# Weighting the last two thirds of a modulation on ScalarE and GpSimd instead of TensorE

## The chip, the cores and the metric

One core of one Trainium2 chip. The metric is device time in microseconds, the median over the runs shown. Engines are named as in the profile: PE (TensorE, matmuls; PEld its weight loads), DVE (VectorE), ACT (ScalarE), POOL (GpSimd), SP (SyncE, which issues most of the DMAs).

## The reference

One layer of a decoder trunk over 512 tokens of width 1024. A condition vector `c` gives six rows of 1024 numbers, the modulation; three token mixers (MLA, sliding window, NSA) run on the modulated, normalised input, then an output projection, a normalisation, and a mixture of 16 experts with two chosen for each token.

```python
cond = jax.nn.silu(c)
mod = cond @ ada_w[l] + ada_b[l]                 # (1, 6144); ada_w is (1024, 6144) f32
sh1, sc1, gt1, sh2, sc2, gt2 = jnp.split(mod[:, None, :], 6, axis=-1)
h = (_ln(x) * (1.0 + sc1) + sh1)
y = concat(o_a, o_b, o_c) @ w_out[l]             # MLA, window, NSA on h @ w_in
x = layernorm(ALPHA * x + (1.0 + gt1) * y, ln1_g[l], ln1_b[l])
h = (_ln(x) * (1.0 + sc2) + sh2)
y = moe(h, router_w, router_bias, ...)
x = layernorm(ALPHA * x + (1.0 + gt2) * y, ln2_g[l], ln2_b[l])
```

Counted in twelve blocks of 512 columns, blocks 0 to 3 are sh1 and sc1, 4 and 5 gt1, 6 and 7 sh2, 8 and 9 sc2, 10 and 11 gt2. Blocks 0 to 3 are needed at once; the change is about blocks 4 to 11, 16 MB of `ada_w`.

## The kernel before

Everything is f32 on tiles of 128 partitions. The program is a straight line without loops on the chip. A scheduler orders the instructions of each engine ahead of time, by the order in which they are written and by hand-set offsets of priority (the table PRM; `pri("st0")` and so on); on the chip each engine and each DMA queue then works its list strictly in order.

The work runs in this order: load x, normalise, transpose (to about 50 us); the first third of the modulation (lines 371 to 388); projections and MLA attention (`keysA`, `latA`, `mla`; about 50 to 130 us), with the projections C1 (`c1`) and B2 (`keys`) between; compression of NSA's keys (`cps`); window attention (`swa`); NSA attention (`queries`, `nsa`; about 200 to 345 us) with the output projection of the four token tiles (`outproj`, yps) between; routing of each tile (`route`, a long chain of small DVE instructions that ends in the table tokB); then four rounds of experts (gu, dn, cmb), whose rows are gathered through tokB by POOL's DMA queue.

The modulation's later blocks are a matrix-vector product on PE. `load_ada` brings 128 rows by 1024 columns at a time (512 KB) into a slot of the pool zraw, which has five slots that w_in's chunks (B2r, C2r ...), phi, w_out and others share. `gemv` (line 320) multiplies two such halves, each half of 512 columns on a quarter of the array, by a column of `cond` that is padded to 32 columns. A DVE addition (lines 537, 548) adds the bank to a row tile. Blocks 4 to 7 are `mod_steps` with four steps, blocks 8 and 9 two more steps of `mod_half`, blocks 10 and 11 two steps of `mod_half` again (`gsteps`). The steps of `mod_steps` are placed between MLA's tiles (line 674, five of the six) and in the order of NSA (s1, the sixth); `gsteps` run at line 1274, behind the output projection. `mod_cols` turns rows into columns by PE transposes, for sh2 and sc2; `gate_out` adds 1 to the gate rows and writes them to DRAM, from where `gate_in` spreads them over all partitions.

Of the kernel before, what the change touches and what calls it, by code (L numbers as in the profile page):

```python
# [10 lines left out]
F32 = mybir.dt.float32  # L11
# [3 lines left out]
OP = mybir.AluOpType  # L15
# [28 lines left out]
T, D, NT, KD = 512, 1024, 4, 8  # L44
# [64 lines left out]
def build(tc, A, out, dbg=None):  # L109
    nc = tc.nc  # L110
    V, S, G, PE, SP = nc.vector, nc.scalar, nc.gpsimd, nc.tensor, nc.sync
# [28 lines left out]
    with top:  # L140
# [3 lines left out]
        cst = top.enter_context(tc.tile_pool(name="cst", bufs=1))  # L144
# [6 lines left out]
        def wraw(name):  # L151
            return zraw.tile([128, 1024], F32, name=name, tag="w")

        def bank(tag, name, bufs=None):
            return psp.tile([128, 512], F32, name=name, tag=tag, bufs=1 if tag in "oq" else 2)
# [4 lines left out]
        gt_d = dram.tile([4, 512], F32, name="gt_d")  # L160
# [23 lines left out]
        for n in range(NT):  # L184
            SP.dma_start(x0[n], xv[:, n])

        def load_ada(i, k, half=(0, 1)):
            t = []
            for a in half:
                t.append(wraw(f"ada{i}_{k}{a}"))  # L190
                c = 2048 * i + 1024 * a
                SP.dma_start(t[-1], A["ada_w"][k * 128:(k + 1) * 128, c:c + 1024])
            return t

        w_in = A["w_in"].rearrange("(k p) c -> p k c", p=128)

        def raw_half(name, hf, ranges):
# [47 lines left out]
        ident = C("id")  # L245
# [66 lines left out]
        def together(calls):  # L312

            head = calls[0]()
            with tc.issue_after(head.ins), tc.high_priority():
                for c in calls[1:]:
                    head = c()
            return head

        def gemv(ps, tiles, first, last):  # L320
            def one(j):
                k, t = tiles[j // 2]
                return lambda: PE.matmul(ps[32 * j:32 * j + 32], cond[:, k], t[:, 512 * (j % 2):512 * (j % 2) + 512],  # L323
                                         start=first, stop=last, skip_group_check=True)


            together([one(j) for j in (2, 0, 1, 3)])

        def mod_bias(i, n=4):
            r = cst.tile([128, 512], F32, name=f"mod{i}", tag=f"mod{i == 8}", bufs=1)  # L330
            V.memset(r, 0.0)
            SP.dma_start(r[0:32 * n:32], A["ada_b"][i:i + n])
            return r

        def mod_cols(i, r):
            ps = bank("t", f"modt{i}")
            for s in range(4):
                PE.transpose(ps[:, s * 128:(s + 1) * 128], r[:, s * 128:(s + 1) * 128], ident)
            c = cst.tile([128, 4, 4], F32, name=f"modc{i}")
            V.tensor_copy(c, ps.rearrange("p (s q) -> p q s", s=4)[:, 0:128:32, :])  # L340
            return c

        def gate_out(i, r):
            V.tensor_scalar(r[0:64], r[0:64], 1.0, None, op0=OP.add)
            SP.dma_start(gt_d[2 * i:2 * i + 2], r[0:64:32])

        def gate_in(i, dst):
            SP.dma_start(dst, gt_d[2 * i:2 * i + 2].rearrange("(o a) c -> o (a c)", o=1).to_broadcast([128, D]))
# [178 lines left out]
        wukv = mp.tile([128, 512], F32, name="wukv", tag="wv")  # L527


        m1, m2 = mod_bias(4), mod_bias(8, 2)  # L530

        def mod_steps():
            for k in range(0, KD, 2):
                ps = bank("z", "modps1")
                for kk in (0, 1):
                    gemv(ps, [(k + kk, t) for t in load_ada(1, k + kk)], kk == 0, kk == 1)
                V.tensor_tensor(m1, ps, m1, op=OP.add)
                yield
            yield from mod_half(m2, 0)

        def mod_half(r, a):

            for k in range(0, KD, 4):
                ps = bank("z", "modps2")
                for kk in (0, 2):
                    gemv(ps, [(k + kk + i, load_ada(2, k + kk + i, (a,))[0]) for i in range(2)], kk == 0, kk == 2)
                for h in range(2):
                    V.tensor_tensor(r[0:64], ps[64 * h:64 * h + 64], r[0:64], op=OP.add)
                yield

        steps = mod_steps()

        def step(n, it=steps):
            for _ in range(n):
# [118 lines left out]
            with pri(f"st{n}"):  # L673
                step(pr(f"stn{n}", 1))
        chB2 = load_chunk("B2", (672, 928))
        mc1 = mod_cols(1, m1)
        gate_out(0, m1)
        zc = {"k": kp.tile([128, 16, 32], F32, name="zck"), "v": kp.tile([128, 16, 32], F32, name="zcv")}
        for kv in "kv":
            src = kr if kv == "k" else vc  # L680
# [289 lines left out]
                load_wo(a, b, wol[a][:, b])  # L970
        gt1 = wraw("gt1")
        gate_in(0, gt1)
        m3 = mod_bias(10, 2)
        gsteps = mod_half(m3, 1)

        def gstep(n):
            step(n, gsteps)
# [27 lines left out]
            return dst  # L1005


        ones = rp.tile([128, 128], F32, name="ones")
        V.memset(ones, 1.0)
        step(16)  # L1010
        mc2 = mod_cols(2, m2)
        V.tensor_scalar(mc2[:, 0:2], mc2[:, 0:2], 1.0, None, op0=OP.add)
        sc2 = lambda k: mc2[:, k // 4, k % 4:k % 4 + 1]
        sh2 = lambda k: mc1[:, 2 + k // 4, k % 4:k % 4 + 1]

        rwm = yp.tile([128, 2, KD, 16], F32, name="rwm")
        rw_ = rwm[:, 1]
# [4 lines left out]
        shr = rp.tile([128, 16], F32, name="shr")  # L1022
        rb05 = rp.tile([128, 16], F32, name="rb05")
        V.tensor_scalar(rb05, rbias, 0.5, None, op0=OP.add)
        for a, mc in enumerate((mc2[:, 0:2], mc1[:, 2:4])):
            V.tensor_tensor(rwm[:, a], rw_, mc.rearrange("p a b -> p (a b)")[:, :, None].to_broadcast([128, KD, 16]),
                            op=OP.mult)
        ps = bank("s", "rsum")
# [243 lines left out]
            G.memset(r, 0.0)  # L1272
        cnt_w = [0]
        step(16, gsteps)
        gate_out(1, m3)
        gt2 = wraw("gt2")
        gate_in(1, gt2)
        lg2 = ep.tile([128, D], F32, name="lg2", bufs=1)
# [266 lines left out]
```

## Time and profile before

| | |
|---|---|
| median of 3 runs | 598.21 us (597.69 to 601.78) |
| profiled execution, device time | 595.62 us |
| its span | 593.8 us |
| TensorE clock granted, mean | 0.97 |
| DMA moved in the span | 117.05 MB |

The span runs from the first to the last recorded instruction; the device time also holds what lies around it. A busy PE is a PE with a matmul in flight. A row of the timeline has start, duration, engine, line, operation; "x8" is a count of records, and an f32 matmul leaves two records.

### The profile page before, as it was taken

To read this page: it belongs to the slowest core of one execution; us is meant where nothing else is said; L and a number is where in the kernel's file an instruction comes from. 1 tells how busy PE (TensorE), PEld (TensorE's weight loads), DVE (VectorE), ACT (ScalarE), POOL (GpSimd) and SP (SyncE) were. 2 spreads that over 40 slices of the span, in tenths; PEclk is the share of its full clock that TensorE was granted. 3 is DMA by queue.
4 is the path that set the end of the run, shared out by engine and by line. 5 is a ranking of instruction groups with operands and counts; after the bars stand their busy time and mean duration, and the time that the engine had idled before them with its cause. 6 is when DMAs were issued, how large, how long until landed. Compare 5 with 4: busy or idle time off the path is not lost.

```text
span 593.8 us, 10447 instructions
## 1 busy us (share of the span) xinstructions
PE 546.8 (92%) x3856; PEld 328.6 (55%) x3856; DVE 367.4 (62%) x1218; ACT 221.8 (37%) x556; POOL 97.5 (16%) x114
## 2 busy tenths in 40 slices
PE   2899999999799999999899999788899999999990
PEld 1469675687698988754455456554334334234240
DVE  7635566654778569877769388885036266157274
ACT  2533543651447336475644412140442071070130
POOL 0214200000000010005101112231501222010123
PEclk9879999999899999999999999987999999999995
DMA  8994137834921100196300794558699999999601
GB/s 302 372 326 170 53 115 273 259 108 145 314 74 40 68 2 2 44 221 202 106 2 1 248 311 149 172 181 285 184 372 354 375 360 342 383 351 340 229 2 47
DMA packets 77546, 117.05 MB, mean 197 GB/s; under 512 B 7937, under 2 KB 54440, under 8 KB 77492
## 3 DMA queue, kind: packets, MB, share of 16 engines
q1 hardware_dynamic: 72328, 102.60, 53.2%
q0 software_dynamic: 4960, 13.64, 6.5%
q8 instruction: 32, 0.52, 0.4%
q14 instruction: 22, 0.18, 0.1%
q10 hardware_dynamic: 204, 0.11, 0.1%
HBM read 112.12 MB, written 8.40 MB: 203 GB/s over the span
## 4 chain that ended last, share of the span: by engine, by line
PE 76%; DVE 9%; DMA 5%; issue 4%; POOL 2%; ACT 2%; ACTq 0%; POOLq 0%
PE gu L1319 13%; PE zps L407 12%; PE dn L1367 7%; PE onsa L894 6%; PE yps L1215 5%; DMA ada<-in_ada_w_dram 3%; PE modps L323 3%; PE zall L423 3%; PE gTp L997 2%; PE stp L501 2%; PE sps L921 2%; PE cmb L1409 2%; PE modps L375 2%; PE wps L849 1%; PE warm L356 1%
## 5 line engine op out<-in xcount | busy, mean ns | idle before, releaser
L1319 PE MATMUL gu<-gu,gT 128*32 128x512 f32 x768 | 87.8, 604 | 0.1
L1319 PEld LDWEIGHTS gu<-gu,gT 128*32 128x32 f32 x768 | 23.2, 110 | 51.1 <-issue 47.9
L1367 PE MATMUL dn<-dn,aT 128*32 128x512 f32 x384 | 45.3, 597 | 0.4 <-ACT aT L127 0.2
L1002 ACT ACTIVATE gT<-gTp,modc,modc 128x128 f32<-128x128 f32 x96 | 35.6, 459 | 9.7 <-PE gTp L997 9.2
L1343 DVE TENSOR_TENSOR act<-act,gu 128x256 f32<-128x256 f32 x12 | 5.0, 421 | 52.4 <-ACT act L1342 52.4
L1215 PE MATMUL yps<-wol,oM 128*128 128x512 f32 x64 | 30.9, 595 | 0.0
L1342 ACT ACTIVATE act<-gu 128x256 f32<-128x256 f32 x12 | 4.6, 387 | 66.1 <-PE gu L1319 66.1
L1373 DVE SCALAR_TENSOR_TENSOR y<-dn,tab,gt 128x512 f32<-128x512 f32 x24 | 18.0, 749 | 16.9 <-PE dn L1367 16.4
L323 PE MATMUL modps<-ada,cond 128*32 128x512 f32 x128 | 18.3, 631 | 5.0 <-DMA ada<-in_ada_w_dram 4.9
L1367 PEld LDWEIGHTS dn<-dn,aT 128*32 128x32 f32 x384 | 10.3, 109 | 20.9 <-issue 16.2
L894 PE MATMUL onsa<-pt,vs 128*64 128x512 f32 x40 | 20.6, 614 | 0.0
L491 ACT ACTIVATE Sg<-Sg,nms 128x128 f32<-128x128 f32 (+3 forms) x32 | 17.8, 559 | 3.7 <-DVE nms L490 3.5
L491 ACT ACTIVATE W<-W,nmw 128x256 f32<-128x256 f32 (+1 forms) x32 | 15.3, 477 | 9.7 <-DVE nmw L490 9.3
L997 PEld LDWEIGHTS gTp<-cf,rows 128*128 128x128 f32 x96 | 10.4, 142 | 15.1 <-ACT gT L1002 9.2
L1389 ACT ACTIVATE R<-R,rsf 128x1024 f32<-128x1024 f32 x3 | 3.7, 1241 | 40.3 <-DVE rsf L1388 40.3
L448 DVE TENSOR_TENSOR rp<-zps,trig 128x128 f32<-128x128 f32 (+1 forms) x28 | 9.7, 346 | 12.6 <-PE zps L407 12.1
L997 PE MATMUL gTp<-cf,rows 128*128 128x128 f32 x96 | 14.8, 282 | 1.7 <-DMA rows<-xs_d,tokB 1.7
L356 PEld LDWEIGHTS warm<-cf 128*128 128x128 f32 x88 | 12.8, 207 | 6.3 <-issue 5.5
L127 ACT COPY pt<-stp 128x512 f32<-128x512 f32 x14 | 7.9, 586 | 22.2 <-PE stp L501 21.9
L356 PE MATMUL warm<-cf 128*128 128x128 f32 x88 | 16.1, 309 | 0.1
L407 PE MATMUL zps<-B1s,hH 128*128 128x256 f32 x64 | 14.1, 312 | 2.2 <-DVE B1s L210 1.1
L1377 DVE TENSOR_TENSOR ys<-y,ys 128x512 fp32r<-128x512 f32 x22 | 15.1, 686 | 1.0 <-ACT ys L127 0.7
(523 smaller groups left out, 1467.6 us busy)
## 6 DMA issues: line engine op xcount, KB each, us to landing
ada<-in_ada_w_dram SPq DMA_DIRECT2D x48, 512.0 KB, 5.9
gu<-in_moe_w_gate_dram SPq DMA_DIRECT2D x32, 512.0 KB, 9.7
gu<-in_moe_w_up_dram SPq DMA_DIRECT2D x32, 512.0 KB, 9.6
dn<-in_moe_w_down_dram SPq DMA_DIRECT2D x16, 1024.0 KB, 10.5
x<-in_x_dram SPq DMA_DIRECT2D x4, 512.0 KB, 5.1
phik<-in_nsa_phi_k_dram SPq DMA_DIRECT2D x4, 512.0 KB, 5.1
phiv<-in_nsa_phi_v_dram SPq DMA_DIRECT2D x4, 512.0 KB, 4.8
wo<-in_w_out_dram SPq DMA_DIRECT2D x8, 256.0 KB, 9.4
```

Source lines behind the costliest of these rows:

```text
L323: return lambda: PE.matmul(ps[32 * j:32 * j + 32], cond[:, k], t[:, 512 * (j % 2):512 * (j % 2) + 512], start=first, stop=last, skip_group ...
L356: PE.matmul(ps[:, :128], ident, ident, start=True, stop=True)
L407: PE.matmul(ps[:, :w], l[:, k, ts_], get(k, r), start=(k == 0 and i == 0), stop=(k == KD - 1 and i == 2))
L423: m = PE.matmul(outs[n], l[:, k, n * 128:(n + 1) * 128], get(k, r), start=(beg and n % 2 == 0), stop=(k == KD - 1 and i == 2), skip_group_ ...
L491: S.activation(S_h, S_h, AF.Exp, bias=nm, scale=-1.0, accum_out=den)
L894: PE.matmul(ops[64 * g:64 * g + 64, cols], lhsT, rhs, start=first[g], stop=False, skip_group_check=True)
L997: PE.transpose(ps[:, k * 128:(k + 1) * 128], src[:, (4 * a + k) * 128:(4 * a + k + 1) * 128], ident)
L1002: S.activation(dst[:, kk], pk, AF.Identity, bias=sh2(kk), scale=sc2(kk))
L1215: last = PE.matmul(ps, l, r[:, cs], start=(i == 0), stop=(i == len(order) - 1))
L1319: together([lambda e=e: PE.matmul(gu[b][32 * e:32 * e + 32], gT[b][:, k, 32 * e:32 * e + 32], w[:, e], start=(k == 0), stop=(k == KD - 1), ...
L1367: together([lambda e=e: PE.matmul(dn[b][32 * e:32 * e + 32], aT[b][:, f, 32 * e:32 * e + 32], w[:, e], start=(f == 0), stop=(f == 1), skip ...
L1373: V.scalar_tensor_tensor(y, dn[b], tab[:, s:s + 1], gt2[:, cs], op0=OP.mult, op1=OP.mult)
```

## The change

Blocks 4 to 11 each become a `mod_block`. A block's rows of `ada_w` come as four tiles (two groups of 128 rows by 512 columns, 512 KB). ACT multiplies each group in place by its 128 numbers of the condition, one for each partition; POOL adds it to an accumulator `acc` of 128x512, which begins as zero with the bias in its first row. After eight groups PE sums `acc` over the partitions: for blocks 6 to 9 with the accumulator as weights and one column of ones (four matmuls, the result is columns, and sc2 gets its 1 here), for the gates with 32 columns of ones as weights (one matmul, the result is a row, to which DVE adds 1 and which SP writes to DRAM). The two accumulators alternate. The six steps of the first generator are blocks 4 to 9, those of `gsteps` blocks 10 and 11; where they stand in the program, and the PRM table, are unchanged. `load_ada`, `gemv`, `mod_bias`, `mod_cols`, `gate_out` and `mod_half` go.

```diff
+        ones = cst.tile([128, 128], F32, name="ones")
+        V.memset(ones, 1.0)
+        mcs = cst.tile([128, 4, 4], F32, name="mcs")
+
+        def mod_block(i):
+            acc = cst.tile([128, 512], F32, name=f"mod{i}", tag=f"mod{i % 2}", bufs=1)
+            G.memset(acc, 0.0)
+            SP.dma_start(acc[0:1], A["ada_b"][i:i + 1])
+            for k in range(0, KD, 2):
+                t = wraw(f"ada{i}_{k}").rearrange("p (a c) -> p a c", a=2)
+                SP.dma_start(t, A["ada_w"][k * 128:(k + 2) * 128, 512 * i:512 * i + 512].rearrange("(a p) c -> p a c", a=2))
+                for a in range(2):
+                    S.mul(t[:, a], t[:, a], cond[:, k + a, 0:1])
+                    G.tensor_tensor(acc, t[:, a], acc, op=OP.add)
             ps = bank("t", f"modt{i}")
...
+            if 6 <= i < 10:
+                for s in range(4):
+                    PE.matmul(ps[:, s:s + 1], acc[:, s * 128:(s + 1) * 128], ones[:, 0:1], start=True, stop=True)
+                V.tensor_scalar(mcs[:, i - 6], ps[:, 0:4], float(i >= 8), None, op0=OP.add)
+            else:
+                PE.matmul(ps[0:32], ones[:, 0:32], acc, start=True, stop=True)
+                V.tensor_scalar(acc[0:1], ps[0:1], 1.0, None, op0=OP.add)
+                r = 2 * (i >= 10) + i % 2
+                SP.dma_start(gt_d[r:r + 1], acc[0:1])
...
-        m1, m2 = mod_bias(4), mod_bias(8, 2)
...
+        def mod_steps(*blocks):
+            for i in blocks:
+                mod_block(i)
                 yield
...
+        steps = mod_steps(4, 5, 6, 7, 8, 9)
...
-        mc1 = mod_cols(1, m1)
-        gate_out(0, m1)
...
-        m3 = mod_bias(10, 2)
-        gsteps = mod_half(m3, 1)
+        gsteps = mod_steps(10, 11)
...
         step(16, gsteps)
-        gate_out(1, m3)
```

## Rows read from the trace of the kernel before

**Rows 1.** Parts 1 and 4 of the page, whole span.
```profile
PE 546.8 (92%) x3856; PEld 328.6 (55%) x3856; DVE 367.4 (62%) x1218; ACT 221.8 (37%) x556; POOL 97.5 (16%) x114
...
PE 76%; DVE 9%; DMA 5%; issue 4%; POOL 2%; ACT 2%; ACTq 0%; POOLq 0%
```

**Rows 2.** Windows, line 323 (gemv) alone: stretch and length, PE busy, PEld busy.
```profile
57.00:117.00 60.00, 11.48 (x80) 1.82 (x80) 1.00 0.52 178
246.00:250.00 4.00, 1.92 (x16) 0.42 (x16) 1.00 0.05 12
380.00:394.00 14.00, 4.93 (x32) 0.81 (x32) 0.88 0.78 281
```

**Rows 3.** Windows: PE, PEld, DVE, ACT, POOL busy, granted clock, DMA, GB/s.
```profile
57.00:117.00 60.00, 59.03 (x400) 39.42 (x399) 37.79 (x120) 26.58 (x79) 6.32 (x10) 1.00 0.52 178
...
275.00:320.00 45.00, 43.33 (x196) 24.37 (x195) 35.23 (x122) 20.30 (x53) 11.14 (x6) 1.00 0.19 59
...
380.00:416.00 36.00, 28.70 (x204) 16.12 (x203) 26.51 (x132) 6.92 (x14) 9.12 (x12) 0.86 0.74 245
```

**Rows 4.** DVE groups by form, 57 to 117 us: busy, mean ns, idle before.
```profile
L537 DVE TENSOR_TENSOR mod<-modps,mod 128x512 f32<-128x512 f32 x4 | 2.8, 692 | 3.8 <-PE modps L323 3.7
...
L452 DVE TENSOR_TENSOR qpd<-rp,rp 128x256 f32<-128x256 f32 x4 | 1.7, 426 | 0.1
...
L576 DVE TENSOR_SCALAR gat<-gat 128x24 f32<-128x24 f32 x1 | 0.2, 178 | 0.0
```

**Rows 5.** Groups by form of ACT and POOL, whole span.
```profile
L131 ACT ACTIVATE Sg<-Sg,dns 128x512 f32<-128x512 f32 x2 | 1.4, 717 | 0.5 <-DVE ymv L1207 0.5
...
L1196 POOL TENSOR_TENSOR ol<-oN,oh 128x512 fp32r<-128x512 f32 x4 | 5.1, 1270 | 40.2 <-PE wps L849 18.7 <-ACT oh L127 11.9 <-ACT th L1068 9.6
```

**Rows 6.** Timeline, 376 to 426 us: start, duration, one sum and one gemv group.
```profile
392.17 1.06 PE L323 MATMUL modps<-ada,cond 128*32 128x512 f32 x8
...
397.57 0.30 PEld L1251 LDWEIGHTS lsum<-cf,x1T 128*128 128x128 f32 x2
```

**Rows 7.** Timeline of POOL and DVE from 398 us, and line 1142's durations (min/median/max).
```profile
398.09 1.86 POOL L1272 MEMSET rows<- 128x1024 f32 x2
...
402.12 0.54 POOL L1328 MEMSET x1g<- 128x512 f32 x1
...
398.62 4.07 DVE L1142 TENSOR_SCALAR aff<-th 128x16 f32<-128x16 f32 x1
...
L1142 DVE TENSOR_SCALAR aff<-th x4: 164/168/4073, 347.6 to 398.6; 128x16 f32<-128x16 f32 x4
```

**Rows 8.** Timeline from 274 us, and line 865's durations (min/median/max).
```profile
274.51 2.35 POOL L985 TENSOR_TENSOR wol<-wo,woh 128x1024 fp32r<-128x1024 f32 x1
...
275.42 1.60 DVE L865 TENSOR_TENSOR sc<-sc,dc 128x128 f32<-128x128 f32 x1
...
L865 DVE TENSOR_TENSOR sc<-sc,dc x4: 284/290/1598, 228.6 to 312.5; 128x128 f32<-128x128 f32 x4
```

**Rows 9.** POOL's part of line 394, durations (min/median/max).
```profile
L394 POOL TENSOR_SCALAR hT<-hT,modc x2: 1386/3314/5242, 27.7 to 43.9; 128x512 f32<-128x512 f32 x2
```

**Rows 10.** SP: timeline from 50 us, and its waits (total, times, longest).
```profile
51.99 58.09 SPq L192 DMA_DIRECT2D ada<-in_ada_w_dram  x20
110.17 2.70 SPq L202 DMA_DIRECT2D B2r<-in_w_in_dram  x2
...
SPq L345 <- DVE mod L344: 27.8, 2, 14.9
```

**Rows 11.** DVE groups by form, 275 to 320 us.
```profile
L133 DVE TENSOR_SCALAR W<-W,rw 128x256 f32<-128x256 f32 x8 | 2.7, 345 | 0.0
...
L858 DVE TENSOR_SCALAR mx<-mx 128x8 f32<-128x8 f32 x1 | 0.1, 150 | 0.0
```

**Rows 12.** Timeline of PE, 380 to 416 us.
```profile
387.59 1.94 PE L323 MATMUL modps<-ada,cond 128*32 128x512 f32 x8 [4.57 <-DMA ada<-in_ada_w_dram]
...
413.65 0.61 PE L1129 MATMUL tabp<-rh,ohp 128*128 128x12 f32 x4
```

More of the change, by code (lines that the diff above doesn't have):

```diff
@@ L185, in build @@
             SP.dma_start(x0[n], xv[:, n])
[L187 to L193, printed above, removed]
         w_in = A["w_in"].rearrange("(k p) c -> p k c", p=128)
@@ L318, in together @@
             return head
[L320 to L333, printed above, removed]
@@ L335, in mod_cols @@
-        def mod_cols(i, r):
-            ps = bank("t", f"modt{i}")
[L337 to L345, printed above, removed]
+        ones = cst.tile([128, 128], F32, name="ones")
@@ L527, in build @@
         wukv = mp.tile([128, 512], F32, name="wukv", tag="wv")
-        m1, m2 = mod_bias(4), mod_bias(8, 2)
[L532 to L537, printed above, removed]
-                yield
[L539 to L551, printed above, removed]
+        def mod_steps(*blocks):
+            for i in blocks:
+                mod_block(i)
+                yield
+        steps = mod_steps(4, 5, 6, 7, 8, 9)
         def step(n, it=steps):
@@ L1005, in tr_mod @@
             return dst
-        ones = rp.tile([128, 128], F32, name="ones")
-        V.memset(ones, 1.0)
         step(16)
[L1011 to L1014, printed above, removed]
+        sc2 = lambda k: mcs[:, 2 + k // 4, k % 4:k % 4 + 1]
+        sh2 = lambda k: mcs[:, k // 4, k % 4:k % 4 + 1]
         rwm = yp.tile([128, 2, KD, 16], F32, name="rwm")
@@ L1024, in build @@
         V.tensor_scalar(rb05, rbias, 0.5, None, op0=OP.add)
-        for a, mc in enumerate((mc2[:, 0:2], mc1[:, 2:4])):
+        for a, mc in enumerate((mcs[:, 2:4], mcs[:, 0:2])):
             V.tensor_tensor(rwm[:, a], rw_, mc.rearrange("p a b -> p (a b)")[:, :, None].to_broadcast([128, KD, 16]),
```

## The prediction

> **What bounds the kernel now.** I read part 1 of the page first: PE is busy for 92% of the span, DVE for 62%, ACT for 37%, POOL for 16%; the chain that ended last runs through PE for 76% of the span [rows 1]. So PE work is what a change should remove, and ACT and POOL look free. The table of windows then says where that is true. The modulation sits in three places: 11.48 us of PE between 57 and 117 us (the MLA stage), 1.92 us at 246 to 250, 4.93 us at 380 to 394 [rows 2]. In the first PE is busy 59.03 of 60 us, DVE 37.79, ACT 26.58, POOL 6.32; between 275 and 320, where the last four blocks' rows begin to be loaded, 43.33 of 45 and DVE 35.23; between 380 and 416 PE has only 28.70 of 36 and DVE 26.51: there routing and its latency bound, not PE [rows 3].
>
> **What goes.** 16 groups of gemv, 18.33 us of PE [rows 2], and the DVE sums that empty their banks: four in the MLA stage before 110 us and two behind, 0.692 us each, 4.1 us [rows 4]; two more at 247 us and four at 383 to 396. The eight transposes of the old mod_cols are small and not counted.
>
> **What comes.** On ACT 64 multiplications of 128x512 by a column, SBUF to SBUF: line 131 has that form at 717 ns, so 45.9 us. On POOL 64 additions of 128x512: line 1196 takes 1270 ns, so 81.3 us, and eight clears of 128x512 at 0.54 us, 4.3 us [rows 5, 7]. On PE 16 sums with one moving column. Nearest is lsum with 16 columns, whose two weight loads take 0.30 us: 4.8 us in all; an estimate between half of that (one load hidden behind the matmul before) and twice (load and matmul in a row). And four row sums of 512 columns with 32 weights columns: eight records, four calls side by side, take 1.06 us; alone one is between a quarter of that and all of it. I take all, since nothing runs beside it: 4.2 us [rows 6]. PE's net relief is 18.33 - 4.8 - 4.2 = 9.3 us, half of what the diff suggests.
>
> **MLA stage, engine by engine.** Blocks 4 to 8 fall here: 40 multiplications, 40 additions, five clears. PE: 59.03 - 11.48 + 12 x 0.30 + 2 x 1.06 = 53.3 us of 60. ACT: 26.58 + 40 x 0.717 = 55.3 us. POOL: 6.32 + 40 x 1.27 + 5 x 0.54 = 59.8 us of 60, before any waiting: POOL becomes the longest engine of this stage [rows 2, 3, 5, 6, 7].
>
> **POOL and DVE wait for each other.** At 274.51 us POOL starts a 2.35 us subtraction, which ends at 276.86. DVE's product of two SBUF tiles at 275.42 takes 1.60 us and ends at 277.02; its median is 290 ns [rows 8]. So DVE waited until POOL was nearly done. The same happens to a tiny tensor_scalar, SBUF to SBUF: median 168 ns, 4073 ns at 398.62, while POOL cleared tiles from 398.09 to 402.66 [rows 7]. The other way about, POOL's 128x512 tensor_scalar takes 5242 ns once and 1386 ns once [rows 9]. The Trainium skill has this as an exclusive lock (SBUF — State Buffer, Who interferes with whom): a DVE instruction with two SBUF inputs, or in a two-port mode, and a GpSimd instruction that reads SBUF block each other fully, the first to issue goes first. By that rule the added POOL work isn't free even where POOL is idle, and the trace agrees with the rows just named.
>
> In the MLA stage 33 DVE instructions read only SBUF tiles, in 13 groups from qpd x4 to gat x1 [rows 4]. With POOL adding for 50.8 of 60 us (0.85), and a wait of half an addition (0.64 us) on average, they wait 33 x 0.85 x 0.64 = 18 us; nothing if they always hit gaps, twice that if each arrives as an addition starts. DVE: 37.79 - 4.1 + 18 = 51.7 us. So four engines stand at 52 to 60 of 60 us where only PE stood there before, and each works its list in order: a multiplication on ACT that waits for a late load stands ahead of the next exp.
>
> What is late next: the 20 loads of the old 20 halves went out from 51.99 to 110.1, B2's rows right behind, at 110.17, since all use the five slots of zraw [rows 10]. The new 20 tiles free their slots at POOL's pace. The 17th, whose slot B2 needs, is done after 17 x 2.54 + 4 x 0.54 + 6.32 = 51.7 us of POOL, plus some 33 x 0.3 = 10 us in which DVE holds the ports: 57 + 61.7 = 118.7, so B2 is 8.5 us late. B2's matmuls are what fills PE's gaps there, and those of the projection before it (C1) run out 11.48 - 5.7 = 5.8 us sooner. The relief of 5.8 us is thus spent on waiting, and what B2 no longer does inside MLA's last gaps moves behind the stage. Sum: +4 us, from -6 (all relief kept) to +16 (relief lost, DVE's 18 us wholly on the chain).
>
> **Block 9 and the wait at 247.** 1.92 us of PE goes, 1.2 comes; eight additions fall in a stage with PE cover. 0 us.
>
> **Blocks 10 and 11.** Before, the first four tiles are loaded early but multiplied at 381 only, since PE is full. On ACT and POOL they run when loaded, and so free the slots for the second block: I expect all 16 additions between 275 and 320. 20.3 us of POOL on 45 is 0.45; 41 DVE instructions there use SBUF alone (from W x8 to mx x1) [rows 11], and wait 41 x 0.45 x 0.64 = 12 us. DVE would be at 35.23 + 12 = 47 of 45 us, so it can't all be hidden; PE's cover is the output projection. +5 us, from 0 to +12. If they run late instead, these 20 us of POOL stand ahead of the gathers that the experts wait for; that is in the range.
>
> **The tail, 380 to 416.** Gone: a wait of 4.57 us for ada on PE, in front of the last tile's transposes [rows 12]; four DVE sums of 0.69 us [rows 4]; SP's wait for the gate row (with the other such wait 27.8 us, twice) [rows 10]. But the chain there is DVE's routing, and tabp ran at 413.65 [rows 12] behind weights and warm-up matmuls in PE's list, which stays. I take DVE's 4 x 0.69 = 2.8 us. -3 us, from 0 to -9.
>
> Sum: +4 + 0 + 5 - 3 = +6 us. The profiled execution took 595.62 us, of which 593.8 us is the span; the median of the runs is 598.21, 2.6 us above. On the median: 604.
>
> **Rivals.**
> *Relief wins (faster).* The waits on the ports fall where PE has cover, POOL keeps pace, and B2 isn't late. Then -6 in MLA, +2 at 275 to 320, -9 in the tail: 598 - 13 = 585. For it: PE's 92% and the 4.57 us wait in the tail; DVE is idle 22 of 60 us in the MLA stage. Against: POOL's 59.8 us of 60. It decides from the point where B2's load goes out before about 112 us.
> *Gain and loss cancel.* The same terms with MLA at 0, the later stage at +3, the tail at -3: 598.
> *Whole trains (much slower).* DVE doesn't get in between two POOL additions and waits for a block's eight. For it: the 4073 ns row, where five ends of clears passed before DVE went on [rows 7]. Against: those clears overlap, while an addition needs the sum of the one before and so leaves a gap. Half of a block (8 x 1.27 / 2 = 5 us) for each of five blocks in MLA and about one of the later ones: 30 us, less 6 of relief: 622. It is the lock of the skill's page with no turn-taking, which the page leaves open.
>
> **How the numbers follow.** Slower by these waits 0.42, with 0.10 of it still within 1%; relief 0.30, with 0.03 within; cancelled 0.18, all within; trains 0.10. A difference of about 1% (6 us) is what a measurement of this kernel can tell from none. Faster 0.27, same 0.31, slower 0.42. The range, 586 to 622, leaves out the better half of the relief case and the worse half of the trains; the likeliest case alone is 598 to 613.
>
> **What would show it.** Right: 128x512 additions on POOL of 1.3 us and more on average, DVE instructions of the 33 at 0.5 us and more, B2's first load after 112 us, POOL near full from 57 to 120 us. Wrong: DVE's mean durations unchanged, or B2 on time with PE idle nowhere; then it is the relief case. Blocks 10 and 11 on POOL after 380 us would put the loss in the tail.

## The result: 636 us, 6.6% slower, and where the trace loses it

The changed kernel takes 636.18 us in the median of 4 runs (631.78 to 639.64), the kernel before 597.95 (4 runs beside it); ratio 1.0658, 95% interval 1.0616 to 1.0700. I had predicted 604, with a range of 586 to 622. The direction was right, the size was not: 38 us instead of 6.

Parts 1 and 4 of the page after, to hold against [rows 1]:

```profile
PE 557.3 (88%) x3760; PEld 344.0 (54%) x3760; DVE 386.3 (61%) x1206; ACT 261.1 (41%) x620; POOL 186.3 (29%) x186
...
PE 65%; DVE 17%; DMA 5%; ACT 4%; issue 4%; POOL 4%; SPq 0%; ACTq 0%; POOLq 0%; DVEq 0%
```

PE has fewer instructions and yet 10.5 us more busy time (546.8 before), and its granted clock was lower (0.93 in the mean instead of 0.97; a zps matmul with B1s takes 329 ns instead of 312). The rest is idle time: 635.9 - 557.3 = 78.6 us, against 593.8 - 546.8 = 47.0. The costliest groups of the page say that the prices of the new work were right (ACT 717 predicted, POOL 1270):

```profile
L327 POOL TENSOR_TENSOR mod<-ada,mod 128x512 f32<-128x512 f32 x64 | 84.4, 1319 | 50.2 <-ACT ada L326 31.6
...
L326 ACT ACTIVATE ada<-ada,cond 128x512 f32<-128x512 f32 x64 | 43.3, 715 | 19.3 <-DMA ada<-in_ada_w_dram 17.9
```

When the same events happen in both traces shows where the time goes. The last step of hL on GpSimd starts 2.5 us later (49.19, 51.66 us); the two loads of E1, the last of w_in, are issued 38.0 us later (157.78, 195.77); the experts' first weights 38.2 us later (326.48, 364.72); the end is 42.1 us later. So nearly everything is lost between hL and E1, in the MLA stage and the compression behind it. Before, then after:

```profile
49.19 1.28 POOL L395 TENSOR_TENSOR hL<-hT,hH 128x512 fp32r<-128x512 f32 x1
157.78 1.50 SPq L202 DMA_DIRECT2D E1r<-in_w_in_dram  x2
```

```profile
51.66 1.29 POOL L389 TENSOR_TENSOR hL<-hT,hH 128x512 fp32r<-128x512 f32 x1
195.77 1.50 SPq L194 DMA_DIRECT2D E1r<-in_w_in_dram  x2
```

The windows of that stretch, first before, then after (PE, PEld, DVE, ACT, POOL busy, granted clock, DMA share, GB/s):

```profile
50.00:75.00 25.00, 24.84 (x169) 18.53 (x168) 11.72 (x48) 8.87 (x32) 4.83 (x9) 1.00 0.42 143
75.00:100.00 25.00, 24.04 (x165) 16.28 (x164) 17.18 (x56) 9.35 (x26) 1.77 (x2) 1.00 0.48 169
...
120.00:145.00 25.00, 24.11 (x210) 19.20 (x212) 13.85 (x40) 9.31 (x27) 0.00 (x0) 1.00 0.27 85
```

```profile
50.00:75.00 25.00, 13.21 (x90) 11.49 (x89) 6.02 (x14) 12.74 (x22) 17.09 (x14) 0.74 0.64 200
75.00:100.00 25.00, 19.07 (x112) 15.47 (x110) 12.51 (x39) 15.27 (x40) 11.20 (x14) 0.85 0.26 82
100.00:120.00 20.00, 18.48 (x121) 14.42 (x121) 16.19 (x49) 7.05 (x21) 6.23 (x6) 1.00 0.07 19
120.00:145.00 25.00, 20.81 (x118) 13.19 (x117) 14.79 (x38) 17.30 (x43) 17.01 (x15) 0.84 0.44 133
```

No engine is full over this stretch after the change: from 50 to 120 us PE is busy for 50.8 of 70 us (13.21 of 25 in the first window, 18.48 of 20 in the third), DVE for half, and POOL, for which I had computed 59.8 of 60, for 34.5. They wait for each other. Who waits for whom at the start is seen in the timelines of ACT, before and after:

```profile
53.82 0.19 ACT L575 ACTIVATE gat<-zall 128x24 f32<-128x24 f32 x1 [5.48 <-PE zall L423]
```

```profile
59.35 6.08 ACT L326 ACTIVATE ada<-ada,cond 128x512 f32<-128x512 f32 x9 [10.28 <-DMA ada<-in_ada_w_dram]
65.44 1.28 ACT L553 ACT_TABLE_LOAD   x1
66.73 0.19 ACT L553 ACTIVATE gat<-zall 128x24 f32<-128x24 f32 x1
```

and of POOL after:

```profile
60.14 13.24 POOL L327 TENSOR_TENSOR mod<-ada,mod 128x512 f32<-128x512 f32 x10 [7.20 <-ACT ada L326]
73.35 0.54 POOL L478 TENSOR_TENSOR ckvs<-ckvs,half 128x1 f32<-128x1 f32 x1
73.86 7.98 POOL L327 TENSOR_TENSOR mod<-ada,mod 128x512 f32<-128x512 f32 x6
```

Nine multiplications stand in ACT's list ahead of gat, ACT's first instruction on the first tile (a gate that NSA uses later; the MLA chain's own first step on ACT, ckvj, follows it). ACT idles 10.28 us for the first ada load, works 6 us on nine halves of such loads, and gat starts at 66.73 instead of 53.82, ckvj at 68.58 instead of 54.65. Ten additions then stand in POOL's list ahead of the power (0.54 us) that the chain needs next: 73.35 instead of 55.34; the fourth such power is at 96.50 instead of 69.89. SP's queue shows the rest of the stage:

```profile
55.16 27.09 SPq L324 DMA_DIRECT2D ada<-in_ada_w_dram  x13
111.45 0.24 SPq L339 DMA_DIRECT2D gt_d<-mod  x1
113.29 0.24 SPq L321 DMA_DIRECT2D mod<-in_ada_b_dram  x1
117.47 8.75 SPq L324 DMA_DIRECT2D ada<-in_ada_w_dram  x4
...
144.81 0.37 SPq L194 DMA_DIRECT2D B2r<-in_w_in_dram  x1
```

From 82 to 111 us SP issues nothing: it stands at the gate row of block 4, and seven of the stage's 20 loads and B2's are behind it. B2's first load goes out at 144.81 (110.17 before, 118.7 predicted).

So there were four suspects: the places in the lists (ACT, POOL), SP's queue, the ports between DVE and POOL, and the lost PE clock.

### The profile page after: what moved, and what is told of

Same layout as the page of the kernel before. It is cut to its first block, busy times and chain, and to the rows that moved or that the text cites. A ratio compares the mean times of both kernels' runs of the same rounds, so it can differ in the third digit from the quotient of the medians.

```text
span 635.9 us, 10480 instructions
## 1 busy us (share of the span) xinstructions
PE 557.3 (88%) x3760; PEld 344.0 (54%) x3760; DVE 386.3 (61%) x1206; ACT 261.1 (41%) x620; POOL 186.3 (29%) x186
## 4 chain that ended last, share of the span: by engine, by line
PE 65%; DVE 17%; DMA 5%; ACT 4%; issue 4%; POOL 4%; SPq 0%; ACTq 0%; POOLq 0%; DVEq 0%
PE gu L1289 12%; PE zps L401 10%; PE dn L1337 7%; PE yps L1186 5%; PE onsa L870 5%; PE modps L369 2%; DMA ada<-in_ada_w_dram 2%; PE gTp L972 2%; PE zall L417 2%; PE cmb L1379 2%; PE omla L627 1%; ACT ada L326 1%; PE sps L897 1%; PE wps L825 1%; POOL mod L327 1%
## 5 line engine op out<-in xcount | busy, mean ns | idle before, releaser
L327 POOL TENSOR_TENSOR mod<-ada,mod 128x512 f32<-128x512 f32 x64 | 84.4, 1319 | 50.2 <-ACT ada L326 31.6
L1289 PE MATMUL gu<-gu,gT 128*32 128x512 f32 x768 | 85.9, 595 | 0.7 <-ACT gT L977 0.5
L326 ACT ACTIVATE ada<-ada,cond 128x512 f32<-128x512 f32 x64 | 43.3, 715 | 19.3 <-DMA ada<-in_ada_w_dram 17.9
L977 ACT ACTIVATE gT<-gTp,mcs 128x128 f32<-128x128 f32 x96 | 35.6, 460 | 8.6 <-PE gTp L972 8.1
L1186 PE MATMUL yps<-wol,oM 128*128 128x512 f32 x64 | 33.3, 617 | 0.0
L972 PEld LDWEIGHTS gTp<-cf,rows 128*128 128x128 f32 x96 | 10.9, 146 | 14.0 <-ACT gT L977 9.2
L350 PE MATMUL warm<-cf 128*128 128x128 f32 x88 | 17.4, 330 | 0.1
L401 PE MATMUL zps<-B1s,hH 128*128 128x256 f32 x64 | 15.4, 329 | 2.1 <-ACT B1s L201 1.5
L401 PE MATMUL zps<-B2s,hH 128*128 128x256 f32 x64 | 15.5, 327 | 1.3 <-DVE B2s L202 1.3
L350 PEld LDWEIGHTS warm<-cf 128*128 128x128 f32 x88 | 14.3, 228 | 4.0 <-issue 3.1
L554 DVE TENSOR_SCALAR gat<-gat 128x24 f32<-128x24 f32 x4 | 2.3, 570 | 22.8 <-ACT gat L553 22.8
```

Of the source, the lines that this page charges most:

```text
L326: S.mul(t[:, a], t[:, a], cond[:, k + a, 0:1])
L327: G.tensor_tensor(acc, t[:, a], acc, op=OP.add)
L350: PE.matmul(ps[:, :128], ident, ident, start=True, stop=True)
L401: PE.matmul(ps[:, :w], l[:, k, ts_], get(k, r), start=(k == 0 and i == 0), stop=(k == KD - 1 and i == 2))
L972: PE.transpose(ps[:, k * 128:(k + 1) * 128], src[:, (4 * a + k) * 128:(4 * a + k + 1) * 128], ident)
L977: S.activation(dst[:, kk], pk, AF.Identity, bias=sh2(kk), scale=sc2(kk))
```

## Experiments

Each run is read by its whole time and by a stage length: from the start of the last hL step on GpSimd to the issue of E1's two loads, which leaves out how early the kernel got going. A time without a ratio is a single one; those of the kernel before scatter from 593 to 603.

| | time, us | stage, us | what it is |
|---|---|---|---|
| before | 596 to 598 | 108.6 | |
| after | 636.18 | 144.1 | |
| e1 | 624.93 | 135.3 | multiplications behind the MLA chain |
| e2 | 654.04 | 142.3 | SP free of gate rows, clears, bias |
| e3 | 638.11 (1.0735) | 128.0 | e1 and e2 |
| e4 | 600.77 (1.0075) | 109.3 | blocks 10 and 11 alone |
| e5 | 600.08 (1.0067) | 112.8 | before + 40 additions |
| e6 / e7 / e8 | 606.36 / - / 598.52 | 124.4 / 129.7 / 115.6 | e1 with thin additions / multiplications / both |
| e9 / e10 | 633.47 (1.0624) / 622.46 (1.0421) | 105.1 / 102.4 | blocks 4 to 9 moved; 10 and 11 as before |
| e11 | 623.76 | 130.9 | e1, B2 loaded first |
| e12 | 623.22 | 116.5 | e3 with both thin |
| e13 | 631.16 | 136.0 | e1 + idle matmuls |
| e14 | 586.24 (0.9842) | 101.3 | before, gemv thin |
| e17 / e18 | 609.73 (1.0205) / 620.41 (1.0365) | 122.4 / 136.1 | before + both engines' work / + joins |

**e1, the lists ahead of the chain.**

```diff
-        S.copy(mpS, ps)
+        chain.append(S.copy(mpS, ps))
...
-                    S.mul(t[:, a], t[:, a], cond[:, k + a, 0:1])
+                    with tc.issue_after(chain[0].ins):
+                        S.mul(t[:, a], t[:, a], cond[:, k + a, 0:1])
```

> The changed kernel with one edit: the multiplications of blocks 4 to 9 are put behind the copy of mpS in ScalarE's list, the last step of the MLA chain before the first attention tile; the additions follow them on GpSimd. Theory of the lists (the multiplications and additions stand ahead of the chain's small steps while their first rows are still on the way): the first ckvs power is at about 55 us as before the change and not at 73, the last at about 72 and not at 96.5, and the time falls by most of the 22 us that were lost by 100 us, to 614 to 622; some is given back, since the slots of zraw come free later. Theory of the ports (DVE slowed by the additions): the same number of additions meets the same DVE work, so the time stays at 630 or more. Theory of SP's queue (gate rows and clears): the 16 us after 100 us are still lost, 620.

The first power is at 55.14 and the last at 69.70 us: the chain is back in its old place. The time falls by 11 us, not by 22 (one run; it lies 3 us above the 614 to 622 of the theory of the lists). So the lists ahead of the chain are one cause; the same kind of loss then reappears in the attention tiles. All engines of e1 in the order of time, from 83 us:

```profile
83.04 5.17 POOL L328 TENSOR_TENSOR mod<-ada,mod 128x512 f32<-128x512 f32 x4
...
85.67 13.81 SPq L324 DMA_DIRECT2D ada<-in_ada_w_dram  x4
...
88.17 0.99 POOL L448 TENSOR_TENSOR qpd<-rp,rp 128x256 f32<-128x256 f32 x1
...
90.18 1.33 ACT L327 ACTIVATE ada<-ada,cond 128x512 f32<-128x512 f32 x2 [6.24 <-DMA ada<-in_ada_w_dram]
91.42 0.39 ACT L131 ACTIVATE Sm<-Sm,dna 128x128 f32<-128x128 f32 x1
...
92.56 7.74 POOL L328 TENSOR_TENSOR mod<-ada,mod 128x512 f32<-128x512 f32 x6 [3.40 <-ACT ada L327]
...
99.14 1.92 PE L337 MATMUL modt<-mod,ones 128*32 128x512 f32 x2 [4.49 <-POOL mod L328]
...
101.09 0.68 DVE L338 TENSOR_SCALAR mod<-modt 1x512 f32<-1x512 f32 x1 [10.88 <-PE modt L337]
```

This shows the mechanism. A slot comes free at POOL's pace, the load follows, ACT waits 6.24 us for it with the attention's Sm behind in its list; POOL adds; PE waits 4.49 us for POOL's last addition, because the row sum stands in its list; and DVE waits 10.88 us for that sum with the next tile's steps behind. A tie from the side work into each engine of the chain.

**e2 and e3, SP's queue.**

```diff
-            SP.dma_start(acc[0:1], A["ada_b"][i:i + 1])
+            G.dma_start(acc[0:1], A["ada_b"][i:i + 1])
...
+            if i in (4, 5):
+                held.append((i, acc))          # summed ahead of gate_in
...
-        steps = mod_steps(4, 5, 6, 7, 8, 9)
+        steps = mod_steps(6, 7, 8, 9, 4, 5)
```

> The changed kernel with SP's waits taken away: the blocks run in the order 6, 7, 8, 9, 4, 5, the two gate blocks are summed and written to DRAM only ahead of the output projection, and the bias rows are loaded by GpSimd's queue behind the clear. The lists of ScalarE and GpSimd ahead of the MLA chain stay. Theory of SP's queue: B2's first load goes out at about 125 to 130 us and not at 144.8, the phi loads follow 15 us earlier, and the time falls by 10 to 16 us, to 620 to 627. Theory of the lists: the first ckvs power stays at 73 us and the last at 96; what is lost by then stays lost. Theory of the ports: no change, 636.

> Both edits together: multiplications behind mpS in ScalarE's list, no gate row, clear or bias row in SP's way. If the two places explain the loss, the time is within 1% of the kernel before (595 to 606), although all additions and multiplications are still made, in the same stage. If the ports are the cause, it stays above 620. If GpSimd's pace (40 additions of 1.3 us, which start 15 us later now) sets B2's load, then B2 goes out at about 130 us and the time is 610 to 616.

e2 takes SP's long wait away and the stage is 142.3 us instead of 144.1: B2's first load at 149.02. SP stood at the gate row, but the slots behind it weren't free any earlier: now it waits for POOL's additions, once for 36.4 us. With the chain freed too (e3 against e1) it is worth 7.3 us of the stage. Both lose it again later, since the gate rows then stand ahead of w_out in SP's queue (its first load at 343.73 in e2, 233.22 in after); this is a flaw of the edit. I had expected e3 within 1% of before; it isn't, by its stage either.

**e4, blocks 10 and 11 alone.** The diff puts `mod_block` for 10 and 11 into the kernel before.

> One part of the change alone: blocks 10 and 11 are weighted on ScalarE and summed on GpSimd, blocks 4 to 9 stay on TensorE as before the change. The prediction's terms are +5 us between 275 and 320 us and -3 us in the tail: 600. The events of the changed kernel's trace put these blocks at 4 us or less: 596 to 602. If the relief of TensorE by 4.9 us and of its wait of 4.57 us counts: 590.

+4.5 us (95%: 2.8 to 6.1). Two windows answer to [rows 3]:

```profile
275.00:320.00 45.00, 37.95 (x162) 20.88 (x161) 37.44 (x106) 28.34 (x65) 28.98 (x21) 0.97 0.32 98
380.00:416.00 36.00, 27.31 (x189) 16.08 (x187) 27.44 (x141) 8.27 (x15) 10.06 (x13) 0.86 0.55 182
```

The additions run from 290.67 to 317 us, as predicted, and PE is busy there for 37.95 us instead of 43.33. By the two traces 8 us are lost between the first and the last product of NSA with vs (252.2 to 341.9 us before, 250.0 to 347.8 in e4), and 3 are won back from there to the last routing table (72.1 and 68.8 us).

**e5, the ports alone.**

```diff
+            with tc.issue_after(last[0].ins):     # last rope step on GpSimd
+                for _ in range((10, 13, 0, 17)[n]):
+                    G.tensor_tensor(vw, vw, vw, op=OP.add)
```

> The kernel before the change, with 40 additions of 128x512 on GpSimd added (an idle tile, vw, is added to itself, result unused), 10, 13 and 17 of them behind the three steps of the rope that GpSimd does, so that none of its other work has to wait. No change on ScalarE, SP, TensorE, in slots or loads. It costs the ports alone: the same 51 us of additions, between 76 and 132 us. Theory of the ports as predicted (each DVE instruction that reads only SBUF waits half an addition on average, on the chain or covered): DVE's busy time in 75 to 132 us rises by 10 to 18 us and the time by 4 to 16 us, 600 to 612. If the ports make the loss of the variant with the multiplications behind the chain (28 us): 620 or more. If the waits are covered: 596 to 599.

0.67% (0.29 to 1.05): 4 us. The windows, before and e5, and the additions (min/median/max):

```profile
76.00:132.00 56.00, 54.85 (x396) 38.62 (x394) 36.34 (x107) 28.01 (x76) 2.51 (x3) 1.00 0.56 188
```

```profile
76.00:132.00 56.00, 52.41 (x366) 36.02 (x366) 42.72 (x106) 26.00 (x70) 45.80 (x42) 1.00 0.56 185
...
L676 POOL TENSOR_TENSOR vw<-vw x40: 1040/1041/2104, 75.9 to 130.2; 128x512 f32<-128x512 f32 x40
```

POOL adds for 44.5 of 56 us and DVE's busy time, which holds its waits at the ports, grows by only 6.4 us. The ports are real and small.

**e6, e7, e8, thin work.** `[:, 0:32]` in the additions, in the multiplications, in both.

> The variant with the multiplications behind the MLA chain (e1, 624.93 us), with additions of 32 columns in place of 512 on GpSimd, so that most of the sum is left out. Loads, slots, multiplications, clears, sums over partitions and gate rows stay. If the ports and GpSimd's pace make the 28 us that e1 still loses: 600 to 606, and DVE's instructions have their old durations. If ScalarE's multiplications between the attention steps, or waits for loads and gate rows make it: 615 or more.

> The same variant (e1, 624.93 us) with multiplications of 32 columns in place of 512 on ScalarE (most of the weighting is left out), additions in full. If ScalarE's 25.6 us between 75 and 150 us make the loss: 605 or less. If GpSimd's additions and the ports make it: 618 or more.

> Both thin (32 columns each; most of the weighting and of the sum is left out). What is left of the change are its loads, slots, clears, bias and gate rows, sums over the partitions, and the places of 64 short instructions on two engines. If work and ports make the loss: at or under the kernel before, 585 to 597, since TensorE is relieved of the modulation. If waits for loads, clears and gate rows make it: 610 or more.

From e1's stage of 135.3 us, thin additions take 10.9, thin multiplications 5.6, both 19.7. Of the 10.9 about 4 would be ports (the stage of e5 is 4.2 us longer than before); the rest is POOL's pace, by elimination. e7's whole time (1584.68 us) is no measure: with that modulation the routing sends the tokens through more rounds of experts (5456 instructions on PE instead of 3760), so it is read only up to E1. With both thin the kernel is level with before, but TensorE's relief isn't seen: beside e14, which has the relief without the change, e8 is 12 us longer, 3 of them in the experts, and its stage 14.3 (one run of e8; both leave most of the modulation out). So the loads, slots, sums and places of this change cost that much even when its work is short.

**e9 and e10, another place.**

```diff
-    "ORD": "q0 q1 n0 n1 q2 q3 s1 n2 Z n3 ...",   "stn0": 1, "stn1": 1, "stn2": 1, "stn3": 2
+    "ORD": "s1 q0 q1 s1 n0 s1 n1 s1 q2 q3 s2 n2 Z n3 ...",   "stn0": 0, "stn1": 0, "stn2": 0, "stn3": 0
```

> The changed kernel with blocks 4 to 9 moved whole to the stage of the NSA queries, behind the last loads of w_in (about 165 to 260 us), where GpSimd has almost nothing to do and DMA is idle; no step is left in the MLA stage. Same 64 multiplications and additions. Theory of the place (in the MLA stage ScalarE, GpSimd and the five slots hold up a chain and the loads behind them; the work itself is cheap): the loss of 38 us up to 180 us goes, TensorE keeps its relief of 11.5 us there, and the time is 585 to 597. Theory of the work (any 64 additions on GpSimd cost DVE and the chain as much wherever they stand): 610 or more. Rival: the blocks only carry their loss along, since the slots are needed for w_out at 249 us: 600 to 610.

> As the run before (blocks 4 to 9 on ScalarE and GpSimd, moved to 165 to 260 us), with blocks 10 and 11 on TensorE as before the change. Blocks 10 and 11 alone cost 0.75% (e4), so this should be about 4 us under the run before: 581 to 593 by the theory of the place, and then faster than both kernels; 606 or more by the theory of the work.

My theory of the place falls. The MLA stage is now shorter than before (105.1 and 102.4 us), and then the blocks lose it all again. From E1's loads to NSA's first output product (onsa) e10 needs 103.6 us, before it was 84.0; from there to the last one 114.0, before 100.1. Before and e10, from 210 us:

```profile
210.00:250.00 40.00, 39.47 (x298) 33.26 (x298) 31.64 (x150) 16.29 (x60) 3.72 (x5) 1.00 0.01 3
```

```profile
210.00:250.00 40.00, 32.21 (x197) 27.12 (x196) 27.04 (x95) 22.08 (x64) 21.69 (x19) 0.83 0.34 104
...
ACT ada L353 <- DMA ada<-in_ada_w_dram: 12.4, 11, 2.8
...
POOL mod L347 <- PE modt L359: 14.6, 1, 14.6
...
304.31 7.12 SPq L979 DMA_DIRECT2D wo<-in_w_out_dram  x8
```

POOL was idle there before, DMA too, and still it costs: the two lines of waits (e10, 165 to 280 us) are the same ties, ACT for loads and POOL's clear for a sum that stands late in PE's list. The last line is another cause that these runs don't separate: w_out's loads stand behind the blocks' in SP's queue and go out at 304.31 instead of 248.61. That is the rival named above, that the blocks carry their loss along. It can't have made the first 20 us, since in the kernel before the output projection first used w_out at 258 us, but it can have made the later 14.

**e11, B2 first.** `chB2 = load_chunk("B2", ...)` moves ahead of the first attention tile.

> The variant with the multiplications behind the MLA chain (e1, 624.93 us), with the two loads of B2 and their splitting put ahead of the first attention tile, so that no slot, no gate row and no clear stands before them. All blocks stay in the MLA stage. If the lateness of B2 (133.6 and 140.9 us instead of 110) makes the loss by leaving TensorE without fill: B2 is loaded before 75 us and the time falls by 8 to 20 us, to 605 to 617. If the attention chain itself is held up by ScalarE and GpSimd between its steps: 620 or more.

B2 is loaded at 54.26 us, and the time is 623.76, 1.2 us under e1. So the late B2, the step on which I had hung my prediction, was in the main a consequence and no cause (single runs; the stage is 4.4 us shorter).

**e12, SP free with thin work.** e3's edits with `[:, 0:32]`.

> The variant of e3 (multiplications behind the chain, SP free of gate rows, clears and bias rows) with multiplications and additions of 32 columns (most of the weighting and of the sum is left out). Beside e8 (598.52 us) it tells what SP's waits cost when neither ScalarE nor GpSimd is busy. If gate rows and clears in SP's way are what is left there: B2's loads go out before 108 us, the last load of E1 is at 158 us or earlier (164.8 in e8). If not: 164 or later. The gate rows stand late, ahead of w_out, in this variant (18 us lost after 200 us in e2), so it is read up to the last load of E1, and the whole time may be 600 to 615.

B2 at 114.35 us, stage 116.5 against 115.6 in e8: nothing. When the two engines are quick, SP's waits cost the stage nothing. The whole time, 623.22, misses the 600 to 615 I had allowed for the late gate rows: w_out's loads go out at 317.60 here.

**e13 and e14, filling and relief.**

```diff
+        def fill():                                  # e13, at each step
+            ps = bank("z", "fill")
+            for kk in (0, 1): ...                     # 8 x PE.matmul(ps[32*j:32*j+32], cond[:, kk], wukv)
...
+            V.tensor_tensor(m1[:, 0:32], ps[:, 0:32], m1[:, 0:32], op=OP.add)   # e14
```

> The variant with the multiplications behind the chain (e1, 624.93 us), with idle matmuls on TensorE in the number, shape and steps of the old gemv of blocks 4 to 8 (40 calls of 32 weights columns by 512 columns, 11.5 us; the result is not used), so that TensorE has its old filling between the steps of attention and does 11.5 us more work than e1. Theory of the clock (in e1 it stands at 0.50 from 90 to 100 and from 125 to 150 us, after stretches in which TensorE was short of work): the clock stays higher, and the time is the same or falls, to 612 to 625. If the lost clock plays no part, the matmuls cost up to their 11.5 us: 628 to 636.

> The kernel before the change with 32 of 512 columns in the gemv of blocks 4 to 9 and in its sums on DVE (most of the modulation of these blocks is left out); loads, slots, order stay, blocks 10 and 11 are whole. It shows what TensorE's relief is worth by itself: 13.4 us of matmuls go and nothing comes in their place. My prediction counted 5.7 us of it as lost on waits and the rest as a gain: by that count 584 to 590. If the gemv only filled gaps of an attention chain that is set by latency, the time is 593 to 599, and there was nothing to gain from moving it.

e1 and e13, the window in which e1's clock was lowest:

```profile
120.00:145.00 25.00, 19.52 (x72) 11.80 (x72) 13.56 (x31) 16.14 (x37) 17.74 (x17) 0.59 0.40 109
```

```profile
120.00:145.00 25.00, 21.26 (x155) 13.56 (x155) 12.99 (x32) 18.13 (x40) 15.22 (x14) 0.97 0.40 123
```

The filling brings the clock from 0.59 to 0.97 in this window and the kernel is no faster (631.16 against 624.93, one run each; stage 136.0 against 135.3). So filling doesn't pay. It doesn't show that the clock costs nothing: the filling is 11.5 us of work itself, and in e13 the clock fell to 0.50 from 95 to 105 us. That a loss is there without the clock is shown by e17 below (0.98 from 75 to 150 us). How much of the 38 us the clock makes stays open; in the changed kernel PE is busy for 9.60 of the 10 us from 140 to 150 at 0.50. e14 says that the relief alone is worth 9.4 us (0.9842, 0.9786 to 0.9899): PE was a real bound, and the change had something to win. From the last routing table to the end e14 takes 180.0 us and the kernel before 179.8, so the gain isn't from other routing.

**e15 to e18, building the cost up on the kernel before.** `load_two` stands at each of the five steps, with no load, slot or SP in it; e15 and e17 leave the last two lines out.

```diff
+        def load_two(i):
+            acc = ...                                 # vw, vz in turn
+            for k in range(8):
+                ...                                   # tile t: vs, kwS in turn (e15, e16: oM[3], vs)
+                with tc.issue_after(chain.ins):
+                    S.mul(o, t, cond[:, k, 0:1])
+                G.tensor_tensor(acc, t, acc, op=OP.add)
+            PE.matmul(ps[0:32], ident[:, 0:32], flat(acc), start=True, stop=True)
+            V.tensor_scalar(flat(acc)[0:1], ps[0:1], 1.0, None, op0=OP.add)
```

> The kernel before the change, whole, with 40 multiplications on ScalarE and 40 additions on GpSimd added in the places of the steps of blocks 4 to 8 and behind the MLA chain, on idle tiles (two tiles multiplied in turn, each added to an accumulator; the result is not used). TensorE keeps its gemv; no load, slot, clear, sum over partitions or gate row is added. Against e5 (additions alone: +4 us) it shows what the multiplications in ScalarE's list and their tie to the additions cost. If it is the work on the two engines in the list of an attention chain that makes the loss: 612 to 630. If the tie to loads and slots makes it (ScalarE waits for a load, the load for a slot, the slot for GpSimd): 598 to 608.

> As the run before, with the gate row's two instructions behind each eight additions: the row sum on TensorE and DVE's addition of 1 to a row, both in the lists of engines that the attention chain needs; no load, no SP. In e1 DVE stood 10.9 us and TensorE 4.5 us for one such sum. If these joins make a good part of the loss: 8 us or more above the run before. If they only end a wait that the chain has anyway: within 4 us of it.

e15 took 615.45 us (1.0339), e16 642.09 (1.0763). Both are spoilt: half of the multiplications fall on oM of the last tile, and the last two blocks of them stood until 145 us behind that tile's attention output, which they change. The next two repeat them on idle tiles.

> As e15, but on tiles that are idle until after this stage (vs and kwS multiplied in turn, vw and vz as accumulators), since in e15 the last sixteen multiplications were made on oM of the last tile and so stood behind that tile's output at 145 us (and changed it). Nothing of the computation is changed here. If the 40 multiplications in ScalarE's list, tied to the additions, hold up the attention chain: qpd of the last tile at 115 us or later (108.8 before), time 608 to 616. If the loss of e15 came from the sixteen late ones: 600 to 605.

> As the run before, with the row sum on TensorE and DVE's addition of 1 to a row behind each eight additions (e16 on idle tiles; nothing of the computation is changed). If TensorE and DVE stand for GpSimd's sums: 6 us or more above the run before, with waits of DVE for the sum of 8 us and more in total between 75 and 150 us. If e16's 27 us came from the two late blocks: within 4 us of the run before.

Windows from 75 to 150 us of before, e17, e18 and e1:

```profile
75.00:150.00 75.00, 72.35 (x564) 51.73 (x562) 44.93 (x134) 31.45 (x83) 2.51 (x3) 1.00 0.54 181
```

```profile
75.00:150.00 75.00, 62.21 (x432) 41.93 (x431) 44.31 (x113) 55.15 (x120) 54.93 (x43) 0.98 0.44 143
```

```profile
75.00:150.00 75.00, 62.15 (x377) 41.19 (x375) 39.97 (x106) 50.86 (x111) 50.75 (x41) 0.91 0.40 132
```

```profile
75.00:150.00 75.00, 57.06 (x281) 37.78 (x279) 43.05 (x101) 50.71 (x111) 54.33 (x45) 0.71 0.46 134
```

e17 costs 12 us, e18 22 (each to some 5 us). 40 multiplications and additions of 29 and 53 us, on engines that were idle for 43 and 72 of these 75 us, take 10 us of PE's work out of the stage though nothing on PE depends on them. One tie of e17 isn't in the real blocks: it multiplies two tiles in turn, so a multiplication can't begin before the addition that still reads its tile. ACT stood 13 us for that (75 to 150 us):

```profile
L618 ACT ACTIVATE vs<-vs,cond 128x512 f32<-128x512 f32 x20 | 14.5, 724 | 5.8 <-POOL vw L619 4.1 <-POOL vz L619 1.5
L618 ACT ACTIVATE kwS<-kwS,cond 128x512 fp32r<-128x512 f32 x20 | 14.4, 722 | 7.4 <-POOL vw L619 4.5 <-POOL vz L619 2.9
```

In the real blocks the way back goes from the addition through slot and load. So e17 gives the price of the work with a short way back, not of multiplications alone.

The joins add 10 more, and the waits of e18 show two ways. The accumulator is held until the sum is done, so POOL stands, with the rope of the next tile behind it in its list; and DVE stands for a sum that is late in PE's list, with the compression's steps (zck at 157.7 us, 149.6 in e17) behind it:

```profile
POOL vw L619 <- DVE vw L622: 7.9, 1, 7.9
...
POOL vz L619 <- DVE vz L622: 6.2, 1, 6.2
...
154.84 0.68 DVE L622 TENSOR_SCALAR vz<-dmy 1x512 f32<-1x512 f32 x1 [7.56 <-PE dmy L621]
```

I had expected 8 us and more of such waits of DVE before 150 us; there are 3.5 by then, and 11.7 by 160.

## Why the prediction was wrong

**The account, by whole times.** Relief -9.4 (e14); ports +4 (e5); the multiplications in ACT's list, tied to the additions both ways, +8 (e17 less e5); joins and held accumulators +10 (e18 less e17); blocks 10 and 11 +4.5 (e4); multiplications and additions ahead of the MLA chain +11 (after less e1). That is 28 of 38 us. The remaining 10 are what no term holds: what only the real blocks have (loads that wait for slots, ACT that waits for loads, clears, gate rows in SP's way), and the lower clock. No run has either by itself, so this rest is argued and not shown, and the parts overlap (e2 gains nothing alone, its edit is worth 7 us of the stage beside e1's), so the account is good to some 5 us a term.

**The step that failed** is the MLA term, +4 with a bound of +16; it measured 35.5 us (144.1 - 108.6 of stage). I added up each engine's work (53.3, 55.3, 51.7 and 59.8 of 60 us), found that all fit, and charged only the wait at the ports. That treats the engines as parallel capacity. I wrote that "each works its list in order: a multiplication on ACT that waits for a late load stands ahead of the next exp", and gave it no price. What the runs showed in its place are waits in these lists: 11 us for the places ahead of the chain (e1), 8 and 10 for the ties within it (e17, e18). The trace before had what a price needs: the attention is a chain that passes between PE, DVE and ACT every microsecond or so and reaches POOL at most once for a tile, and the blocks' ties from one list into the next (load to ACT and ACT to POOL for each multiplication, POOL to PE and PE to DVE for each block) put a possible stop into each of these lists. An upper bound would have been the time that the blocks need as a chain of their own, 40 x 1.27 = 51 us, an estimate that no run tests.

**The ports**: mechanism right, size wrong. DVE's kpr step (before 216 ns) after the change:

```profile
L446 DVE TENSOR_TENSOR kpr<-rp,rp x4: 215/1059/1085, 68.5 to 85.1; 128x64 f32<-128x64 f32 x4
```

That is its own 0.22 us and a wait of 0.84, less than one addition: DVE gets in between two additions. The longest wait of the DVE steps that I had counted is 1.09 us, of a qpd (1508 ns, 418 before). The rival of whole trains is refuted; that its 622 was the nearest number is luck. Of the 18 us of waits 6.4 came (e5), and 4 reached the end. The Trainium skill's rule (SBUF — State Buffer, Who interferes with whom), that such DVE and GpSimd instructions block each other and the first to issue goes first, agrees with these rows; it leaves open who goes next after an instruction, and that DVE does is what makes it cheap here. The 4073 ns of [rows 7] are no case of the rule as I put it, which speaks of GpSimd instructions that read SBUF: those were clears, which only write.

**The late B2**: the direction was right (after 112 us), the value (118.7) wrong, and its role too: it follows from the late chain for the most part (e11).

**The relief**: I let 5.8 us of it be spent on waiting; alone it is real (e14), so the rival "relief wins" was right about PE and wrong about the price of the new work.

**Blocks 10 and 11**: +5 - 3 = +2 predicted, +4.5 measured (by the events of one trace +8 and -3), in the place and at the time predicted. The reason I gave for their late turn before, a full PE, was not it: gsteps stand behind the output projection in PE's list. **Block 9**: not told apart. Of the four signs I had named, three held (additions 1.32 us, B2 late, DVE's steps over 0.5 us, these only in some groups: kpr 0.85, gat 0.57, but kr 0.29); "POOL near full from 57 to 120 us" was wrong, and was the one that mattered: POOL was not short of time, it stood in line.

## What to carry to other kernels

A share of 16% busy on an engine isn't free capacity when its list also carries small steps of a latency chain: what counts is which step of the chain stands behind each added instruction, and what that instruction can wait for. Price moved work by its ties (each wait from one in-order list into another) as well as by its microseconds: with short work the same ties cost 20 us of stage less (e8 against e1). The late loads and the lower clock that one sees in the trace afterwards may be consequences. Cheap tests are to add the work without its purpose to the old kernel (e5, e17, e18) and to take it away without a substitute (e14).

## What the runs showed of the hardware

DVE and POOL take turns between back-to-back additions: 40 additions, 44.5 us of POOL, cost DVE 6.4 us (e5), and no DVE step that I had counted waited longer than 1.09 us in the changed kernel, where an addition takes 1.32. An addition of 128x512 with the same tile as both inputs takes 1.04 us (e5), with two tiles 1.26 us and more. And the clock granted to PE stayed at 0.50 (1.2 GHz) in e1 from 125 to 150 us though PE was busy for 4.9 of 5 us in part of it; it had fallen after a stretch of 2.42 busy us in 5:

```profile
120.00:125.00 5.00, 2.42 (x9) 1.48 (x9) 4.69 (x14) 4.89 (x13) 2.74 (x4) 0.93 0.03 10
...
130.00:135.00 5.00, 4.91 (x24) 3.07 (x24) 0.42 (x1) 1.36 (x3) 3.38 (x3) 0.50 0.69 200
```
